# Softmax probabilities copied into a float32r tile by a transfer, and transposed from there

## The chip, the cores and the metric

One core of a Trainium2 chip runs the whole program. Its engines have queues of their own: PE (matrix products and transposes), DVE (VectorE), ACT (ScalarE), POOL (GpSimd), and SP, which in this kernel does nothing but start transfers. The metric is the device time of one execution in microseconds. Instructions of one engine run in the order in which they were built; between engines, semaphores hold them.

## The reference

Two layers of a decoder trunk over 512 tokens of width 1024, batch 1, in float32. In each layer a combined projection feeds three groups of attention heads; their normalised outputs go through one output projection; a SwiGLU feed-forward part and a gated per-layer embedding follow. What the change touches is the softmax of two groups, eight sparse heads (two branches each, over selected blocks and over a window) and four forgetting heads:

```python
def masked_softmax(logits, mask):
    l = jnp.where(mask, logits, NEG_INF)
    m = jnp.max(l, axis=-1, keepdims=True)
    e = jnp.where(mask, jnp.exp(l - m), 0.0)
    return e / jnp.maximum(jnp.sum(e, axis=-1, keepdims=True), TINY)
...
        p_s = masked_softmax(s_s.reshape(b, g_, hpg, tq, n_sel * NSA_SLC_LEN), mask_s)
        o_s = jnp.einsum('bghtnk,bgtnkd->btghd', p_s.astype(vs.dtype), vs)
...
        p_w = masked_softmax(s_w, mask_w)
        o_w = jnp.einsum('bghtk,bkgd->btghd', p_w.astype(vw.dtype), vw)
        o = gt[..., 0:1] * o_c + gt[..., 1:2] * o_s + gt[..., 2:3] * o_w
...
        p = masked_softmax(logits, s_idx[None, :] <= t[:, None])
        return jnp.einsum('bhts,bshd->bthd', p.astype(v.dtype), v)
```

## The kernel before

Float32 products run as passes over operands split into two float32r tiles: a high part (the value rounded to float32r) and the remainder, so that hi x hi, hi x lo and lo x hi add up to nearly float32. Weights come from DRAM as raw tiles (`wraw`, three buffers), ACT writes the high part and DVE or POOL the remainder (`halves`, lines 197 to 201) into `whl` (five buffers).

The attention of a layer is written as generators that are woven with projections, each at its share of the other's progress: the first group of four sparse heads runs beside the query projection of the second and two projections of the forgetting heads, the second group beside further projections and the first part of the output projection, the forgetting heads beside more of the output projection. A scheduler in the tile framework then fixes the order on each engine by priority and by its own estimate of when things are ready; nothing is reordered at run time.

`softmaxes(items)` (line 752) holds the three steps of an item, which is a query tile of 128 rows with one to four softmaxes side by side over at most 512 columns:

- `scores`: PE makes the scores in a PSUM bank and adds the mask (lines 766 and 768). DVE takes the maximum (L771), ACT the exponential with its sum (L774) into a tile `p` (six buffers), DVE the reciprocal of the sum (L776, L777), and POOL scales the row with it and with the branch's gate (L779). The tile `p` is float32.
- `transposes`: PE transposes the blocks of 128 columns of `p` into one PSUM bank `pTp`, one to four of them (L787); ACT writes the high part from there (L792) and DVE the remainder (L793).
- `values`: PE multiplies what is there with v (L983 for the sparse heads, L839 for the forgetting ones).

A loop calls them so that the scores of an item stand three steps ahead of its transposes, and these two steps ahead of its products with v:

```python
            look, lag = 3, 2
...
            for st in range(n + look + lag):
                if st < n:
                    yield scores(items[st])
                if 0 <= st - look < n:
                    yield transposes(items[st - look])
                if 0 <= st - look - lag < n:
                    it = items[st - look - lag]
                    yield it["values"]() if it["values"] else 0
```

A layer has 60 items: 22 for each group of sparse heads, 16 for the forgetting heads. All transfers are started from SP's queue, in its order: the weights, the small vectors, and the swaps `sw` (lines 451 and 452), which copy a head's stack of queries or keys within SBUF with its two halves of 64 partitions exchanged. In the same kernel PE transposes float32r tiles too, the stacks of queries and keys, through the float32r identity `identr` (L442, PSUM tile `stk`).

Of the kernel before, what the change touches and what calls it, by code (L numbers as in the profile page):

```python
# [19 lines left out]
P = 128  # L20
# [13 lines left out]
SCRATCH = 1024     # Pool starts no DMAs  # L34
LN_EXP = "natural_log_exp_and_others"

# Columns of the input projection.
# [5 lines left out]
def hybrid_trunk_kernel(  # L43
# [8 lines left out]
    """float32 products run as three float32r passes over operands split exactly into a high part  # L52
    (the float32r rounding) and the remainder: hi*hi + hi*lo + lo*hi. Where both halves fit on the
    partitions of one operand, the fourth product comes along."""
# [3 lines left out]
    def bc(ap, n):  # L58
        """A row of DRAM on all partitions."""
        return bass.AP(tensor=ap.tensor, offset=ap.offset, ap=[[0, P], [1, n]])  # L60

    def f(ap):
        return ap.bitcast(F32)
# [12 lines left out]
    def utile(shape, dt=F32R, name="u"):  # L76
        """One of the 8 KiB slots that all larger tensors share."""
        return upool.tile(list(shape), dt, name=name, tag="u", bufs=15)

    class Lazy(dict):  # L80
        """Tiles made when first used, so that slots are taken in the order of use."""
# [24 lines left out]
    # how far ahead of the order of the program: evacuations, norms, the per-layer embedding  # L106
    OFE, OFN, OFP = 100, 50, 200

    def weave(*streams):
        """Trace streams (generator, total work) side by side, each at its share of the others' progress."""  # L110
# [17 lines left out]
    @contextlib.contextmanager  # L128
    def prio(off):
        """What is traced here counts as off instructions earlier in the order of the program."""  # L130
        c = tc.cur_priority
        tc.cur_priority = c - off
        yield
        tc.cur_priority += off

# [72 lines left out]
    def weights(w, kts, c0, c, per):  # L208
        """Row tiles kts (that follow each other) of w[:, c0:c0+c] as [P, (hi, lo), tile, column], `per`
        of them in a tile; yields them one by one."""  # L210
# [16 lines left out]
    def project(act, w, kts, c0, c, evac, tags="ddss", tail=2):  # L227
        """Token-major product of act(k, half, token tile) with w[:, c0:c0+c]: the row tiles of w go
        by once, all token tiles taking part; the last ones token tile by token tile. Columns up to
        256: two token tiles share a bank."""  # L230
# [24 lines left out]
        for tt in range(NT):  # L255
# [9 lines left out]
            # a bank that two tiles share is read when both are whole  # L265
# [5 lines left out]
    def project_rows(act, w, kts, c0, c, evac, tag="d", ws=None):  # L271
        """The same, token tile by token tile, the weights staying."""
# [9 lines left out]
    def project_T(act, w, c0, evac, tags):  # L282
        """256 columns of w, weights stationary: [128 columns, t] twice. The last row tiles bank by bank."""
# [22 lines left out]
    sums, early, latest = {}, {}, {}  # L306
    junk = const.tile([P, 768 + 512], BF16, name="junk")      # nothing reads it
# [9 lines left out]
    def begin_rms(tt, n):  # L317
        """The part of the mean square that the first n columns make, ahead of the rest, and where the gain
        is at hand its product with the first half."""
# [18 lines left out]
    def load_gain(gain):  # L338
        """The next norm's gain on all partitions."""
# [5 lines left out]
    def normed(g):  # L345
        """The halves of the rows of RMSNorm of h."""
        first = last_act[0] is None
        for tt in range(NT):
# [4 lines left out]
            # where the next tile's last products are on their way, they go first  # L353
            act_after, dve_after = (tc.issue_after(x) if tt + 1 in done else ExitStack()
                                    for x in done.get(tt + 1, (None, None)))
            # at the start, what comes in late does not hold up what is there already
# [15 lines left out]
    def norm_T():  # L372
        """RMSNorm of h, transposed, in two parts; as act(k, half, token tile or None for all)."""
# [26 lines left out]
    def rope(acc, c, nh, tt, out, dup=1):  # L400
        """Rotary embedding of nh heads at acc[:, c:]; out [P, nh, (dup,) 64]."""
# [15 lines left out]
    def split_heads(src, nh, scale=1.0):  # L417
        """[P, nh, (hi | lo), 64] of scale * src [P, nh, 64]."""
# [5 lines left out]
    def split_v(src, dst):  # L424
        """dst [P, heads, (hi | lo), 64] of src [P, heads, 64]."""
# [12 lines left out]
    def stack(t, nh, dsts):  # L438
        """Transposes [tok, (hi | lo)] of nh <= 4 heads; dsts: (destination, heads) in turn."""
# [8 lines left out]
    def swap(src):  # L448
        """The stack with its halves exchanged."""
# [5 lines left out]
    # =================== mixer ===================  # L455
    def mixer(i):
# [24 lines left out]
        def compress(which, pos, w1, w2):  # L481
# [38 lines left out]
            # tanh form of gelu: x / (1 + exp(-2u)), u = sqrt(2/pi) (x + 0.044715 x^3)  # L520
# [64 lines left out]
        def head_out(head, o):  # L585
            """o: [(o.hi | o.lo), t]; its two halves are added up."""
# [9 lines left out]
        def pair_out(pr, half, o):  # L596
            """The same for half of the queries of both heads, o: [(o.hi | o.lo), query tile, head, query]."""
# [28 lines left out]
        def sb_heads():  # L626
            # kv tiles, each with its first query and first column, that share a bank
            groups = (((3, 256, 0), (2, 256, 256)), ((1, 128, 0),), ((0, 0, 0),))
            items = []
            for hd in range(4):  # L630
                parts = {}      # kv tile -> its softplus, first query, first column
# [90 lines left out]
        def forget_rows():  # L722
            """Rows that bring c_t - c_s into the scores, c the running sum of log-sigmoid."""
# [589 lines left out]
```

## Time and profile before

| | |
|---|---|
| runs | 1585.79, 1592.13 and 1586.5 us; median 1586.5 |
| span of the profiled execution | 1585.9 us (the time around it isn't listed; the median is 0.6 us above the span) |
| PE busy | 1516.4 us, 96% of the span |
| DVE, ACT, POOL busy | 748.0, 735.1 and 576.4 us |
| transfers | 134.58 MB in 114449 packets |
| softmax attention | about 176 to 340 us in layer 0, 961 to 1122 us in layer 1 |

Busy time of PE is modelled: products are pipelined, and a record's length is more than the time until the next one can start. What a product costs PE is therefore read from start to start, or from the chain of waits, which gives each piece the time up to the next.

### The profile page before, as it was taken

Reading aid. Unit: us, or ns where it says so; the run is one execution under the profiler, and the core shown is the slowest. Engines: PE = TensorE matmul, PEld = TensorE weight load, DVE = VectorE, ACT = ScalarE, POOL = GpSimd, SP = SyncE. Lnnn points to the kernel's source line nnn. Section 1 sums busy time; section 2 is a strip of 40 time slices with the busy share of each in tenths; the row PEclk is TensorE's granted clock in tenths of the full one; section 3 lists DMA queues with packets and bytes.
Section 4 is the critical chain, followed back from the end, with each engine's and each line's share of the span. In section 5 each row is a group of like instructions: output and inputs, shape, how many; then the busy total and the mean of one; then the engine's idle time right before and its main releaser. Section 6 shows DMA issues by size and latency. Waiting matters only on the chain.

```text
span 1585.9 us, 23185 instructions
## 1 busy us (share of the span) xinstructions
PE 1516.4 (96%) x8630; PEld 1286.7 (81%) x8630; DVE 748.0 (47%) x1584; ACT 735.1 (46%) x1561; POOL 576.4 (36%) x636
## 2 busy tenths in 40 slices
PE   6899999999999999999988999999999999999997
PEld 6788887878888888888977988778798888888887
DVE  6677869763111111214366778697711121112153
ACT  5476676654333332323353776586533333323243
POOL 4233455453323333321223134555433333323223
PEclk9999999999999999999999999999999999999999
DMA  5421321132333333332224212211233333333221
GB/s 161 116 75 39 81 69 34 48 94 67 93 95 101 98 93 120 119 94 67 81 69 122 56 50 72 79 29 53 81 94 94 93 94 104 101 113 120 93 68 66
DMA packets 114449, 134.58 MB, mean 85 GB/s; under 512 B 6864, under 2 KB 91936, under 8 KB 114336
## 3 DMA queue, kind: packets, MB, share of 16 engines
q1 hardware_dynamic: 114336, 133.10, 28.6%
q8 instruction: 68, 1.11, 0.3%
q14 instruction: 45, 0.37, 0.1%
HBM read 122.59 MB, written 2.10 MB: 79 GB/s over the span
## 4 chain that ended last, share of the span: by engine, by line
PE 77%; DVE 12%; ACT 3%; issue 3%; POOL 3%; DMA 1%; POOLq 0%; ACTq 0%; DVEq 0%
PE gu L224 10%; PE gu L223 10%; PE gu L222 10%; PE acc L223 6%; PE acc L222 6%; PE acc L224 6%; PE accr L222 3%; PE accr L223 2%; PE sc L766 2%; PE accr L224 2%; PE pTp L787 2%; PE no L983 2%; PE ge L222 1%; PE ge L224 1%; PE ge L223 1%
## 5 line engine op out<-in xcount | busy, mean ns | idle before, releaser
L201 POOL TENSOR_TENSOR whl<-wraw,whl 128x512 fp32r<-128x512 f32 (+2 forms) x248 | 333.2, 1348 | 721.0 <-ACT whl L198 617.3
L198 ACT ACTIVATE whl<-wraw 128x512 fp32r<-128x512 f32 (+2 forms) x416 | 260.7, 630 | 490.0 <-PE gu L224 290.3
L201 DVE TENSOR_TENSOR whl<-wraw,whl 128x512 fp32r<-128x512 f32 x168 | 127.1, 758 | 507.0 <-ACT whl L198 506.5
L224 PE MATMUL gu<-xT,whl 128*128 128x512 f32 (+1 forms) x768 | 287.4, 374 | 0.0
L223 PE MATMUL gu<-xT,whl 128*128 128x512 f32 (+1 forms) x768 | 287.2, 374 | 0.0
L222 PE MATMUL gu<-xT,whl 128*128 128x512 f32 (+1 forms) x768 | 286.8, 373 | 0.0
L223 PEld LDWEIGHTS gu<-xT,whl 128*128 128x128 f32 x768 | 144.2, 188 | 27.5
L224 PEld LDWEIGHTS gu<-xT,whl 128*128 128x128 f32 x768 | 144.2, 188 | 27.4
L222 PEld LDWEIGHTS gu<-xT,whl 128*128 128x128 f32 x768 | 144.4, 188 | 27.1
L223 PE MATMUL acc<-whl,hid 128*128 128x512 f32 x352 | 139.6, 397 | 0.0
L222 PE MATMUL acc<-whl,hid 128*128 128x512 f32 x352 | 139.6, 397 | 0.0
L224 PE MATMUL acc<-whl,hid 128*128 128x512 f32 x352 | 138.8, 394 | 0.0
L779 POOL TENSOR_SCALAR p<-p,rc,gt 128x128 f32<-128x128 f32 (+3 forms) x128 | 79.3, 631 | 70.4 <-DVE rc L777 20.8
L774 ACT ACTIVATE p<-sc,mx 128x128 f32<-128x128 f32 (+3 forms) x160 | 83.9, 536 | 22.3 <-DVE mx L771 20.2
L792 ACT ACTIVATE pT<-pTp 128x512 fp32r<-128x512 f32 (+2 forms) x120 | 62.1, 527 | 40.2 <-PE pTp L787 38.8
L793 DVE TENSOR_TENSOR pT<-pTp,pT 128x512 fp32r<-128x512 f32 (+2 forms) x120 | 70.5, 595 | 21.4 <-ACT pT L792 20.4
L224 PEld LDWEIGHTS acc<-whl,hid 128*128 128x128 f32 x352 | 66.3, 188 | 15.4
L223 PE MATMUL acc<-whl,xT 128*128 128x256 f32 x256 | 73.6, 288 | 5.3 <-DVE whl L201 5.3
L222 PEld LDWEIGHTS acc<-whl,hid 128*128 128x128 f32 x352 | 66.2, 188 | 15.1
L223 PEld LDWEIGHTS acc<-whl,hid 128*128 128x128 f32 x352 | 66.1, 188 | 15.3
L222 PE MATMUL acc<-whl,xT 128*128 128x256 f32 x256 | 74.3, 293 | 2.6 <-DVE sv L427 2.0
L224 PE MATMUL acc<-whl,xT 128*128 128x256 f32 x256 | 74.5, 292 | 0.0
(300 smaller groups left out, 3300.7 us busy)
## 6 DMA issues: line engine op xcount, KB each, us to landing
wraw<-in_w_ffn_gate_dram SPq DMA_DIRECT2D x44, 512.0 KB, 3.8
wraw<-in_w_ffn_up_dram SPq DMA_DIRECT2D x44, 512.0 KB, 3.8
wraw<-in_w_ffn_down_dram SPq DMA_DIRECT2D x44, 512.0 KB, 3.7
wraw<-in_w_in_dram SPq DMA_DIRECT2D x36, 512.0 KB, 3.8
wraw<-in_w_out_dram SPq DMA_DIRECT2D x16, 512.0 KB, 3.7
wraw<-in_w_ple_gate_dram SPq DMA_DIRECT2D x16, 512.0 KB, 3.4
sw<-nq SPq DMA_DIRECT2D x32, 128.0 KB, 2.4
wraw<-in_w_in_dram SPq DMA_DIRECT2D x8, 280.0 KB, 2.9
```

What stands on the lines that cost most here:

```text
L198: se.activation(whl[:, 0], raw[:, lo:lo + n], AF.Copy)
L201: eng.tensor_tensor(whl[:, 1], raw[:, lo:lo + n], f(whl[:, 0]), op=ALU.subtract)
L222: i = te.matmul(acc, lhsT=lh, rhs=rh, start=start, stop=False, skip_group_check=True)
L223: te.matmul(acc, lhsT=lh, rhs=rl, start=False, stop=False, skip_group_check=True)
L224: te.matmul(acc, lhsT=ll, rhs=rh, start=False, stop=stop, skip_group_check=True)
L766: te.matmul(s[:, c:c + w], lhsT=lhsT, rhs=rhs, start=(j == 0), stop=False, skip_group_check=True)
L774: se.activation(e[:, u * n:(u + 1) * n], s[:, u * n:(u + 1) * n], AF.Exp, bias=mx[:, u:u + 1], accum_out=sm[:, u:u + 1])
L779: ge.tensor_scalar(e[:, u * n:(u + 1) * n], e[:, u * n:(u + 1) * n], rc[:, u:u + 1], gates[u] if gates else 1.0, op0=ALU.mult, op1=ALU.mult)
L787: te.transpose(pt[:, kt, :], e[:, kt * P:(kt + 1) * P], ident)
L792: se.activation(hi, src, AF.Copy)
L793: ve.tensor_tensor(lo, src, f(hi), op=ALU.subtract)
L983: te.matmul(o[:, qt % 2], lhsT=nv5[:, g, br, kt].rearrange("p t d -> p (t d)"), rhs=pT[:, j, u, kt], start=False, stop=(br == 1 and kt == ...
```

## The change

The probabilities still arrive in the float32 tile `p`. After POOL's scaling a transfer on SP's queue copies them, word for word, into a new tile `er` of type float32r (two buffers), and the transposes read `er`, with the float32r identity and a float32r PSUM tile. The scores now stand four steps ahead of the transposes. The rest of the diff removes comments, which moves line numbers by three after line 780: the transposes are on L790, their evacuations on L795 and L796, the products with v on L842 and L986.

```diff
-            look, lag = 3, 2
+            look, lag = 4, 2
...
                 for u in range(k):
                     ge.tensor_scalar(e[:, u * n:(u + 1) * n], e[:, u * n:(u + 1) * n], rc[:, u:u + 1],
                                      gates[u] if gates else 1.0, op0=ALU.mult, op1=ALU.mult)
+
+                it["e"] = er = upool.tile([P, 512], F32R, name="er", tag="er", bufs=2)
+                nc.sync.dma_start(f(er[:, :k * n]), e[:, :k * n])
                 return sum(w for _, w, _, _ in prods) + k * P / 2
...
             def transposes(it):
                 nb, e = it["k"] * (it["qt"] + 1), it["e"]
-                pt = bank("t", (P, 4, P), name="pTp")
+                pt = bank("t", (P, 4, P), F32R, name="pTp")
                 for kt in range(nb):
-                    te.transpose(pt[:, kt, :], e[:, kt * P:(kt + 1) * P], ident)
+                    te.transpose(pt[:, kt, :], e[:, kt * P:(kt + 1) * P], identr)
                 hi, lo = it["dst"]()
-                src = pt[:, :nb, :]
+                src = f(pt[:, :nb, :])
```

Outside the softmax attention the order on every engine stays as it was. The first place is PE in the second group of sparse heads of layer 0, around the items of three blocks. Before (`accr` is the output projection, `sc` the scores, `no` the products with v):

```order
L787 MATMUL pTp<-ident,p 128x128 x3
L983 MATMUL no<-pT,nv 128x256
L768 LDWEIGHTS identb
L768 MATMUL sc<-cmaskb,identb 128x128
L223 MATMUL accr<-whl,on_1479 128x512
L766 MATMUL sc<-nk,nq_2193 128x256
L766 MATMUL sc<-nk,sw 128x256
L766 MATMUL sc<-nk,nq_2193 128x256
L766 MATMUL sc<-nk,sw 128x256
L787 MATMUL pTp<-ident,p 128x128 x3
L983 MATMUL no<-pT,nv 128x256 x7
L787 MATMUL pTp<-ident,p 128x128 x3
```

The same items after; the three groups of three blocks are again one item each, and follow one another:

```order
L790 MATMUL pTp<-identr,er 128x128 x3
L986 MATMUL no<-pT,nv 128x256
L224 MATMUL accr<-whl,on_1479 128x512
L766 MATMUL sc<-nk,nq_2224 128x512
L766 MATMUL sc<-nk,sw 128x512
L986 MATMUL no<-pT,nv 128x256 x6
L790 MATMUL pTp<-identr,er 128x128 x3
L986 MATMUL no<-pT,nv 128x256
L768 LDWEIGHTS identb
L768 MATMUL sc<-cmaskb,identb 128x2x128
L766 MATMUL sc<-nk,nq_2224 128x512
L790 MATMUL pTp<-identr,er 128x128 x3
```

The transposes of an item now read `er`, and the scores between them belong to items further ahead. The second place is SP's queue in the same stage. Before, it holds weight loads (`wraw`) and swaps (`sw`) alone; the names in brackets are the semaphores that each waits for (`DMAHW` are earlier transfers):

```order
L194 DMA wraw<-in_w_out_dram 128x2x512 [waits DMAHW7_49,Pool_49]
L194 DMA wraw<-in_w_out_dram 128x2x512 [waits DMAHW0_49,Pool_49]
L194 DMA wraw<-in_w_out_dram 128x2x512 [waits DMAHW4_49,DMAHW1_49,Pool_49]
L451 DMA sw<-fqk_2887 64x512 [waits DMAHW2_49,DVE_49,PE_49]
L452 DMA sw<-fqk_2887 64x512 [waits DMAHW3_49,Activation_49]
```

After, each copy waits for POOL (its probabilities) and for PE (the transposes of the item two before it, out of the same buffer of `er`):

```order
L194 DMA wraw<-in_w_out_dram 128x2x512 [waits Pool_49]
L194 DMA wraw<-in_w_out_dram 128x2x512 [waits DMAHW6_49,Pool_49]
L783 DMA er<-p 128x512 [waits DMAHW2_49,DMAHW7_49,PE_49,Pool_49]
L783 DMA er<-p 128x512 [waits DMAHW4_49,PE_49,Pool_49]
L194 DMA wraw<-in_w_out_dram 128x2x512 [waits DMAHW3_49,DMAHW1_49,Pool_49]
L783 DMA er<-p 128x512 [waits DMAHW7_49,PE_49,Pool_49]
L783 DMA er<-p 128x384 [waits DMAHW0_49,PE_49,Pool_49]
L783 DMA er<-p 128x384 [waits DMAHW2_49,PE_49,Pool_49]
```

Between the weight loads now stand 120 copies over both layers, and ten times in each layer a copy stands directly behind a weight load.

## Rows read from the trace of the kernel before

**Rows 1.** The page: busy time of each engine, and the chain by engine.
```profile
PE 1516.4 (96%) x8630; PEld 1286.7 (81%) x8630; DVE 748.0 (47%) x1584; ACT 735.1 (46%) x1561; POOL 576.4 (36%) x636
...
PE 77%; DVE 12%; ACT 3%; issue 3%; POOL 3%; DMA 1%; POOLq 0%; ACTq 0%; DVEq 0%
```

**Rows 2.** Spans and granted clock of the cores.
```profile
core 0: 1585.9 us, clock 0.993
```

**Rows 3.** Windows: the three softmax stages of layer 0, columns in the first line.
```profile
core 0: us, PE busy (x) PEld busy (x) DVE busy (x) ACT busy (x) POOL busy (x), PEclk, DMA share, GB/s
175.00:225.00 50.00, 49.45 (x362) 43.07 (x362) 39.79 (x121) 36.08 (x95) 29.03 (x38) 1.00 0.23 65
254.00:292.00 38.00, 36.93 (x251) 30.39 (x250) 34.64 (x89) 31.23 (x79) 23.87 (x37) 1.00 0.16 43
297.00:337.00 40.00, 37.67 (x218) 30.93 (x217) 27.86 (x72) 23.93 (x60) 21.54 (x25) 0.98 0.32 93
```

**Rows 4.** Timeline of PE: start, length, what; four transposes amid a stage, then at its end.
```profile
270.76 0.60 PE L787 MATMUL pTp<-ident,p 128*128 128x128 f32 x4
...
335.57 1.12 PE L787 MATMUL pTp<-ident,p 128*128 128x128 f32 x4 [2.33 <-POOL p L779]
```

**Rows 5.** Instructions on tile pTp: count, ns min/median/max, first and last start, forms.
```profile
L787 PE MATMUL pTp<-ident,p x400: 270/273/476, 175.8 to 1119.8; 128*128 128x128 f32 x134
L792 ACT ACTIVATE pT<-pTp x120: 257/583/671, 176.5 to 1120.1; 128x512 fp32r<-128x512 f32 x64, 128x384 fp32r<-128x384 f32 x40, 128x128 fp32r<-128x128 f32 x8, 128x256 fp32r<-128x256 f32 x8
```

**Rows 6.** The chain of waits around eight transposes: start, us up to the next.
```profile
223.88 0.23 PE accT L224
224.11 0.87 PE pTp L787 x8
224.98 0.12 PE no L983
```

**Rows 7.** Instructions on tile stk, the float32r transposes.
```profile
L442 PEld LDWEIGHTS stk<-identr,heads x96: 137/139/146, 109.1 to 978.8; 128*128 128x128 f32 x96
L442 PE MATMUL stk<-identr,heads x96: 222/247/285, 109.2 to 978.9; 128*128 128x128 f32 x96
```

**Rows 8.** Timeline of PE around two groups of four float32r transposes.
```profile
155.12 0.53 PE L442 MATMUL stk<-identr,heads 128*128 128x128 f32 x4
155.49 0.35 PE L222 MATMUL acc<-whl,xT 128*128 128x256 f32 x1
155.68 0.28 PE L223 MATMUL acc<-whl,xT 128*128 128x256 f32 x1
...
192.39 0.46 PE L442 MATMUL stk<-identr,heads 128*128 128x128 f32 x4
192.69 0.35 PE L766 MATMUL sc<-nk,nq 128*128 128x256 f32 x1
192.87 0.28 PE L766 MATMUL sc<-nk,sw 128*128 128x256 f32 x1
```

**Rows 9.** Transfers by line: count, KB each, median us from issue to landing.
```profile
sw<-nq SPq DMA_DIRECT2D x32, 128.0 KB, 2.4
...
wraw<-in_w_in_dram SPq DMA_DIRECT2D x8, 260.0 KB, 2.8
...
sw<-sqk SPq DMA_DIRECT2D x16, 128.0 KB, 2.7
sw<-fqk SPq DMA_DIRECT2D x16, 128.0 KB, 2.3
...
out_dram<-xn SPq DMA_DIRECT2D x4, 256.0 KB, 2.0
```

**Rows 10.** Waits of SP's queue: for whom, us in total, times, longest.
```profile
SPq L194 <- POOL whl L201: 818.6, 189, 23.3
```

## The prediction

> **What bounds the kernel now.** I read the page's busy shares and chain first, then the clock, then the busy time of the attention stages, and last the waits and single instructions in them. PE is busy in 96% of the span and carries 77% of the chain that ended last; no other engine passes 47%, and DMA carries 1% of the chain [rows 1]. The granted clock is 0.993 over the run, so PE is at its upper level, 2.4 GHz, nearly throughout [rows 2]. The change touches only the attention heads with a softmax. There PE is busy for 49.45 of 50.00 us, 36.93 of 38.00 and 37.67 of 40.00 in the three stages of layer 0, and DVE is already at 34.64 of 38.00 in the second [rows 3]. So a nanosecond less on PE is worth nearly a nanosecond there, as long as the probabilities arrive in time. Where they don't, PE stands: at the end of the forgetting heads it waits 2.33 us for POOL's last scaling, and the four transposes after it take 1.12 us where four elsewhere take 0.60, since the clock had dropped to its lower level (the stage's mean is 0.98) [rows 3, 4].
>
> **The change, part by part.** The sum is made against the profiled span of 1585.9 us; the median of the runs shown is 1586.5, so 0.6 us lies around it.
>
> *Transposes.* There are 400, in 64 groups of four (the evacuations of 512 columns), 40 of three, 8 of two and 8 of one [rows 5]. On the chain a run of eight float32 transposes takes 0.87 us, 0.109 each [rows 6], so all 400 take 43.6 us. The float32r form stands in the trace too, in the stacks of queries and keys [rows 7]. Where its inputs are at hand, four take 0.30 us to the start of the next product, and that product then takes 0.18 us to its successor instead of the 0.12 of 256 columns [rows 6, 8]: 0.36 us in all against 0.436. Where they aren't, it is 0.37 plus 0.07, or 0.44: no gain [rows 8]. With some 0.085 us from one to the next I take 0.36, 0.275, 0.19 and 0.105 us for four, three, two and one. The saving is 64 x 0.076 + 40 x 0.052 + 8 x 0.028 = 7.2 us. Bounds: 0 (all like the worse group) to 400 x (0.109 - 0.07) = 15.6 us, if all went at the spacing inside the better group, (0.46 - 0.247) / 3 = 0.07 us [rows 7, 8]. I take 7.
>
> *The copies.* 120 transfers on SP's queue, of 64 to 256 KB. The trace has none of this shape within SBUF; the nearest are 128 KB within SBUF (2.4 us to landing), 260 KB from DRAM (2.8) and 256 KB to DRAM (2.0) [rows 9]. I take 2.5 us for most: a little over the SBUF row, since twice the bytes move. The Trainium skill, "DMA: Bandwidth & Descriptors", section "Anatomy of one DMA — SWDGE (gpsimd) path", has a fixed 2.0 us plus bytes over 436 GB/s (for the GpSimd path), which by estimate is 2.6 us for 256 KB; the SBUF row agrees (2.4 us against 2.3 by the page), the row of 256 KB to DRAM doesn't (2.0). By 2.6 us the ring below would cost some 12 us and the whole sum would come to about 1591 us.
>
> *The ring of two.* The copies go into two buffers, so the copy for an item waits until PE has transposed the item two before it (the PE wait on each copy in the order shown with the diff). From the start of that last transpose to the first new one there pass 0.25 us until it is whole, the copy, and 0.14 us of weight load [rows 7]: 2.9 us with 2.5 for the copy, or 2.8 of other PE work in between. In the PE order shown for the second group there stand, between the groups of three at its two ends, two products with values (0.24 us), one of 512 columns of the output projection (0.23), three of scores (0.69), six more with values (0.72), a group of three transposes (0.28) and a mask (about 0.1): 2.26 us by the durations of [rows 6, 8]. So PE waits there about 0.5 us. Counted alike over both layers, 42 of 108 such stretches are under 2.8 us; adding the shortfalls in turn, each delay also giving time to the copy behind it, makes 9 us (1.5, 1.9 and 1.1 in the three stages of a layer). At 2.0 us to landing it is 1 us, at 2.8 us 18.6. I take 9. Behind a waiting transpose all of PE's work is queued; behind a waiting copy, on SP, the swaps of the next heads and the weight loads.
>
> *Looking four ahead instead of three.* In the built order the scores of an item stand further ahead of its transposes, for the last item of the forgetting heads about twice as far. That should remove most of the 2.33 us wait at the end of layer 0 and the slow clock behind it, and some of the same in layer 1: I take 3 us off (bounds 0, if the copy eats it, and 8).
>
> *The rest.* POOL, ACT and DVE do the same work. The copies add about 26 MB to 134 and stand in stages where the DMA engines are 16 to 32% busy [rows 3], so they cost the weights little. SP's order costs something: ten times in each layer a copy stands directly behind a weight load that waits for POOL. I put 2 us on it; DVE near its limit in the second group is within that (bounds 0 and 25, see the third rival).
>
> *Sum:* -7 + 9 - 3 + 2 = +1 us on the span, so 1587 us for the run.
>
> **The rivals.** *The copies are hidden.* If a copy lands in 2.0 to 2.3 us, the ring costs 1 to 2 us and the sum is -7 + 2 - 3 = -8: 1578 us. For it: 256 KB to DRAM took 2.0 us. Against it: no transfer within SBUF has a median under 2.3, with half the bytes [rows 9]. A branch of it has the float32r transposes at 0.07 us each as well: 8 us more, 1570.
>
> *The ring decides (slower).* Place: the second NSA group, where 12 of 20 stretches are short. Price: with 2.8 us to landing the ring costs 18.6 us, and the longer look saves 1 us instead of 3, so -7 + 18.6 - 1 + 2 = +13: 1599 us. It decides from a landing of 2.7 us on, where it alone costs 15. For it speaks the 260 KB row at 2.8; against it that this row reads DRAM, and in pieces half as large as a copy's, and that a PE that waits elsewhere leaves the ring more time.
>
> *SP's order decides (slower).* Weight loads wait 189 times for POOL, 818.6 us in all, 4.3 each and up to 23.3 [rows 10]. If a third of such a wait falls on the copy behind each of the 20 loads and PE has nothing else, 20 x 1.4 = 28 us replace the ring's 9 and the 2: -7 + 28 - 3 = +18, so 1604 us. Against it: the waits of before are those of a queue that ran ahead, and most loads are ready before the copy behind them has its probabilities.
>
> *Transposes aren't what holds PE.* If DVE's 34.64 of 38 us in the second group [rows 3] sets the pace, neither term counts in full and the time stays at 1585 to 1589; this falls within the forecast.
>
> **How the numbers follow.** Gain and ring nearly cancel: 0.52 for a time between 1579 and 1594. Hidden copies have 0.16, their branch with the faster transposes 0.03, the ring 0.18, SP's order 0.11. A measurement of this kernel can tell about 0.5%, 8 us, from no change; so the first two give 0.19 faster (1578 lies just past that edge), the ring and SP's order 0.29 slower, and 0.52 is left for no change. The forecast's own terms give 1579 to 1594; with the other cases the range is 1574 to 1604, which leaves out the fast branch below and about half of SP's order, with the ring's far end, above.
>
> **What would show it.** Right: the float32r group on line 790 at 0.08 to 0.09 us per transpose on the chain; copies landing in 2.4 to 2.6 us; PE waiting for the copies some 30 to 50 times, each under 1 us, most in the second group; no 2.33 us wait at the end of the forgetting heads. Wrong: copies at 2.0 us and no such waits (faster); copies at 2.8, or SP waiting for POOL with a copy behind it and PE idle for 2 us and more with the clock down (slower); or a transpose spacing of 0.109 as before, which would leave only the costs.

## The result, and the profile after

The changed kernel takes 1607.8 us (median of 4, 1603.7 to 1610.3) against 1588.6 before in the same comparison: ratio 1.0114, 95% interval 1.0097 to 1.0132, so 18 us slower (15 to 21). The forecast was 1587, the range ended at 1604. The profiled execution has a span of 1605.6 us, 19.7 more than before.

The page of the changed kernel, against [rows 1], and its span and clock, against [rows 2]:

```profile
PE 1526.8 (95%) x8630; PEld 1292.4 (80%) x8630; DVE 751.4 (47%) x1584; ACT 737.9 (46%) x1561; POOL 575.1 (36%) x636
...
PE 73%; DVE 12%; ACT 5%; issue 3%; POOL 3%; DMA 3%; POOLq 0%; ACTq 0%; DVEq 0%; SPq 0%
```

```profile
core 0: 1605.6 us, clock 0.985
```

PE has lost four points of the chain, DMA and ACT have gained two each, and the clock is 0.985 instead of 0.993. Windows of the changed kernel that hold the three softmax stages of layer 0 (columns as in [rows 3]):

```profile
177.00:235.00 58.00, 52.57 (x363) 45.17 (x362) 42.36 (x115) 36.18 (x93) 28.67 (x37) 0.94 0.45 146
264.00:302.00 38.00, 35.74 (x234) 29.59 (x234) 32.87 (x87) 29.19 (x74) 21.48 (x30) 0.96 0.43 146
306.00:350.00 44.00, 41.99 (x243) 33.36 (x242) 28.95 (x75) 26.99 (x64) 24.24 (x32) 1.00 0.41 132
```

In the first, PE stands 5.4 of 58 us, where it stood 0.55 of 50, and the clock is 0.94 instead of 1.00. By the timeline, the stretch from the first group's compressed scores to the second's grew from 69.6 to 77.3 us in layer 0 and from 69.6 to 75.5 in layer 1: 13.8 of the 19.7 us. I had put the largest part of the ring's cost, 1.9 of 4.5 us a layer, into the second group.

What PE waited for there: its timeline in the changed kernel (start, length, what, and in brackets the wait and who ended it), which answers to [rows 4]:

```profile
178.85 0.54 PE L790 MATMUL pTp<-identr,er 128*128 128x128 f32 x4 [1.03 <-DMA er<-p]
...
183.43 0.89 PE L790 MATMUL pTp<-identr,er 128*128 128x128 f32 x7 [1.17 <-DMA er<-p]
...
219.13 0.45 PE L790 MATMUL pTp<-identr,er 128*128 128x128 f32 x3 [1.90 <-DVE pT L796]
...
234.74 0.50 PE L790 MATMUL pTp<-identr,er 128*128 128x128 f32 x4 [1.03 <-DMA er<-p]
...
349.20 0.53 PE L790 MATMUL pTp<-identr,er 128*128 128x128 f32 x4 [0.78 <-DMA er<-p]
```

The first two are the first and the third item of the group: their copies left within 0.03 us of POOL's end, so no ring held them, and too little other work covered their landing, which took 2.28 us for the first and 3.38 us for the third, with a weight load started 1.07 us ahead of it. The fourth had a late copy, as the chain of the changed kernel shows (start, us, what):

```profile
230.07 4.53 DMA er<-p
...
234.74 0.50 PE pTp L790 x4
```

The third wait is not for a copy; it comes back below, with e8. The last is the end of the forgetting heads: the 2.33 us of [rows 4] are gone, 0.78 for a copy stand there instead. PE's waits in all (for whom, us, times, longest; before, no line names a copy, and the transposes waited 3.7 us, 4 times, for POOL):

```profile
PE pTp L790 <- DMA er<-p: 8.7, 10, 1.2
...
PE sc L766 <- ACT p L774: 4.6, 4, 2.1
PE pTp L790 <- DVE pT L796: 4.6, 4, 1.9
```

To see the whole loss I added up the start-to-start times of PE's instructions in the attention stages of both layers: what exceeds a product's usual time by over 0.25 us ("standing"), what the lower clock added, and the transposes themselves, in us.

| kernel | standing | of it ahead of transposes | ahead of scores | lower clock | transposes |
|---|---|---|---|---|---|
| before | 16.4 | 7.7 | 6.6 | 1.5 | 35.5 |
| after | 31.7 | 18.8 | 6.1 | 8.1 | 30.6 |
| e7 (no copies, three ahead) | 17.7 | 7.5 | 6.6 | 3.6 | 32.5 |
| e8 (no copies, four ahead) | 25.7 | 7.4 | 9.2 | 6.7 | 31.4 |
| e16 (ring of three) | 29.9 | 16.8 | 8.8 | 4.9 | 31.2 |

After against before: 15.3 more standing, 6.6 more for the clock, 4.9 less for the transposes, 17 of the 19.7 us. The profiled executions are not the median ones: e8's and e16's were the slowest of theirs, e7's the fastest.

The copies by size, against [rows 9], and the waits of SP's queue, against [rows 10]:

```profile
er<-p SPq DMA_DIRECT2D x64, 256.0 KB, 2.3
er<-p SPq DMA_DIRECT2D x40, 192.0 KB, 2.1
```

```profile
SPq L194 <- POOL whl L201: 745.1, 192, 26.2
...
SPq L783 <- PE pTp L790: 105.3, 84, 4.8
SPq L783 <- POOL p L779: 37.2, 29, 7.9
...
SPq L783 <- DMA er<-p: 14.0, 10, 2.2
```

These are waits, and a copy can have more than one: 84 were ended by the ring (PE's transposes out of the buffer), 29 by POOL, 10 by the landing of an earlier copy. Matched copy by copy in the trace, 112 of the 120 left within 0.3 us of the later of their own two conditions, 91 times the ring's and 21 times POOL's. Two stood behind a weight load for about 1 us.

### The profile page after: what moved, and what is told of

The parts are those of the page before. It is cut to its first block, busy times and chain, and to the rows that moved or that the text cites. A ratio compares the mean times of both kernels' runs of the same rounds, so it can differ in the third digit from the quotient of the medians.

```text
span 1605.6 us, 23403 instructions
## 1 busy us (share of the span) xinstructions
PE 1526.8 (95%) x8630; PEld 1292.4 (80%) x8630; DVE 751.4 (47%) x1584; ACT 737.9 (46%) x1561; POOL 575.1 (36%) x636
## 3 DMA queue, kind: packets, MB, share of 16 engines
q1 hardware_dynamic: 131616, 159.32, 31.7%
## 4 chain that ended last, share of the span: by engine, by line
PE 73%; DVE 12%; ACT 5%; issue 3%; POOL 3%; DMA 3%; POOLq 0%; ACTq 0%; DVEq 0%; SPq 0%
PE gu L224 10%; PE gu L223 10%; PE gu L222 10%; PE acc L222 6%; PE acc L223 6%; PE acc L224 6%; PE accr L222 2%; PE accr L223 2%; PE accr L224 2%; DMA er<-p 2%; PE sc L766 2%; PE no L986 2%; PE ge L222 1%; PE ge L223 1%; PE ge L224 1%
## 5 line engine op out<-in xcount | busy, mean ns | idle before, releaser
L223 PEld LDWEIGHTS gu<-xT,whl 128*128 128x128 f32 x768 | 144.2, 188 | 27.5
L774 ACT ACTIVATE p<-sc,mx 128x128 f32<-128x128 f32 (+3 forms) x160 | 83.4, 528 | 25.4 <-DVE mx L771 19.7
L796 DVE TENSOR_TENSOR pT<-pTp,pT 128x512 fp32r<-128x512 f32 (+2 forms) x120 | 71.3, 597 | 34.9 <-ACT pT L795 33.0
L795 ACT ACTIVATE pT<-pTp 128x512 fp32r<-128x512 f32 (+2 forms) x120 | 62.4, 525 | 51.2 <-PE pTp L790 50.1
```

The costliest lines, as they stand in the source:

```text
L223: te.matmul(acc, lhsT=lh, rhs=rl, start=False, stop=False, skip_group_check=True)
L774: se.activation(e[:, u * n:(u + 1) * n], s[:, u * n:(u + 1) * n], AF.Exp, bias=mx[:, u:u + 1], accum_out=sm[:, u:u + 1])
L795: se.activation(hi, src, AF.Copy)
L796: ve.tensor_tensor(lo, src, f(hi), op=ALU.subtract)
```

## The experiments

Eighteen kernels ran. The theories: A, a copy's own time between POOL and PE; B, the ring of two; C, the order that four ahead gives; D, the transposes gain nothing; E, traffic and queue order; F, late landings beside weight loads; G, more in flight. Below, a ratio is to the kernel before on the same chip, whose median moved between 1588.6 and 1590.0; 0.0010 is 1.6 us.

| run | look | transposes | copies, ring | median us | ratio, 95% interval |
|---|---|---|---|---|---|
| e15 | 2 | f32r | none | 1592.2 | 1.0019, 1.0010 to 1.0028 |
| **e7** | 3 | f32r | none | 1581.5 | 0.9956, 0.9939 to 0.9972 |
| e2 | 3 | f32r | 2 | 1610.6 | 1.0129, 1.0114 to 1.0145 |
| e3 | 4 | f32 | none | 1595.0 | 1.0029, 1.0017 to 1.0041 |
| e5 | 4 | f32 | 2, not read | 1596.2 | 1.0047, 1.0033 to 1.0061 |
| e8 | 4 | f32r | none | 1595.9 | 1.0045, 1.0029 to 1.0061 |
| after | 4 | f32r | 2 | 1607.8 | 1.0114, 1.0097 to 1.0132 |
| e16 | 4 | f32r | 3 | 1599.7 | 1.0061, 1.0041 to 1.0081 |
| e17 | 4 | f32r | 4 | 1599.2 | 1.0056, 1.0035 to 1.0077 |
| e12 | 5 | f32r | none | 1596.6 | 1.0050, 1.0035 to 1.0065 |
| e11 | 5 | f32r | 2 | 1615.0 | 1.0176, 1.0154 to 1.0199 |
| e18 | 5 | f32r | 4 | 1599.1 | 1.0062, 1.0042 to 1.0081 |

**The look-ahead alone (e3).**

```diff
-            look, lag = 3, 2
+            look, lag = 4, 2
```

> The kernel before with a look-ahead of four, no copies, float32 transposes. Theory A: the 2.33 us wait at the end of the forgetting heads and the stretch at the lower clock behind it (1.7 us) go, some back for waits on DVE: 1584 to 1589 us. Theory C: the two waits for DVE of 2.1 us are here too, with one stretch at the lower clock each: 1593 to 1597 us.

1595.0 us: by the ratio 4.6 slower (2.7 to 6.5), where I had forecast 3 faster. The wait at the end of the forgetting heads went, as forecast, but another came. From its timeline, and its list of PE's waits (us, times, longest; before: 4.6, 2, 2.3 on the first line, and no second):

```profile
336.08 0.38 PE L839 MATMUL fo<-pT,fv 128*128 128x256 f32 x1 [1.50 <-ACT pT L792]
```

```profile
PE sc L766 <- ACT p L774: 6.7, 8, 2.3
...
PE fo L839 <- ACT pT L792: 2.8, 2, 1.5
```

A fourth item ahead means one more set of scores at the start of a group, and the score banks are three: two of the new waits, 0.56 us each, stand at the start of the first group. The time is theory C's, its waits are not: in place of its two waits of 2.1 us for DVE there is one of 0.5 us. Nor do PE's waits make up the loss. In the softmax stages of both layers they add up to 12.7 us against 11.1 before, since most of the 3.7 us for POOL went, and the lower clock, once more in layer 1, costs about 1.7. These stages are 7.0 us longer in the profiled execution; the other 4 us stay open.

**The transposes alone (e7, e8).** The probabilities' own tile becomes float32r:

```diff
-                it["e"] = e = ptile("p")
+                it["e"] = e = upool.tile([P, 512], F32R, name="p", tag="p", bufs=6)
...
-                    ge.tensor_scalar(e[:, u * n:(u + 1) * n], e[:, u * n:(u + 1) * n], rc[:, u:u + 1],
+                    ge.tensor_scalar(e[:, u * n:(u + 1) * n], f(e[:, u * n:(u + 1) * n]), rc[:, u:u + 1],
...
-                pt = bank("t", (P, 4, P), name="pTp")
+                pt = bank("t", (P, 4, P), F32R, name="pTp")
...
-                    te.transpose(pt[:, kt, :], e[:, kt * P:(kt + 1) * P], ident)
+                    te.transpose(pt[:, kt, :], e[:, kt * P:(kt + 1) * P], identr)
```

> The kernel before, look-ahead of three, no copies; the probabilities' own tile is float32r, so ACT's exponentials and POOL's scaled probabilities are rounded as they are written, and the transposes are float32r. Nothing else changes. Transposes as predicted (7.2 us) or as the changed kernel's trace has them (a group of four 0.366 us against 0.439, a group of three 0.336 against 0.339, some 5 us): 1582 to 1585 us. Theory D, they are hidden behind other engines: 1588 to 1590 us.

> The same with a look-ahead of four: the changed kernel without its copies and without their buffers. If look-ahead and transposes add up: 1595.0 - 4 = 1590 to 1591 us, as far as the run with POOL's own float32r tile (1591.4) was not held back by its four buffers; with that hold gone, down to 1586 us.

With three ahead it is 1581.5 us, 7.0 us faster than the kernel before (4.4 to 9.7) and the fastest of all versions; its probabilities are rounded, so it is not the same computation. In its profiled execution the softmax stages of both layers, from the first group's compressed scores to the forgetting heads' last product, are 5.0 us shorter (345.3 against 350.3); by the table 3.0 of them are the transposes' own time. Where the others are saved isn't shown. From its chain, eight transposes, against 0.87 in [rows 6]:

```profile
223.52 0.23 PE accT L224
223.75 0.63 PE pTp L787 x8
224.38 1.02 PE no L983 x8
```

With four ahead it is 1595.9: no gain over float32 with four ahead (e3). The transposes are as fast, but by the table PE stands 8.0 us more than in e7 and the lower clock takes 3.1 us more, 11 of the 14 us between the two. Its waits in e8, and the head norm of DVE (ns min/median/max):

```profile
PE sc L766 <- ACT p L774: 7.4, 6, 2.4
...
PE pTp L787 <- DVE pT L793: 4.0, 2, 2.0
...
PE no L983 <- DVE pT L793: 3.5, 2, 1.8
...
PE fo L839 <- ACT pT L792: 2.7, 2, 1.6
...
PE pTp L787 <- POOL p L779: 0.5, 3, 0.2
```

```profile
L617 DVE SCALAR_TENSOR_TENSOR pair<-pair,hgT,rs x16: 737/754/3246, 137.1 to 1138.3; 128x512 f32<-128x512 f32 x16
```

POOL's lateness (3.7 us in the kernel before) is nearly gone, which is what the longer look-ahead is for; but once in each layer PE waits 2 us for an evacuation that is queued on DVE behind a norm of 3.2 us (1.4 us at most in the kernel before) and 1.8 us for one behind another DVE instruction of 2.9 us (L857, 0.5 us in the middle of the kernel before), and the forgetting heads end late. The changed kernel has the same two waits, one in each layer. DVE there, then POOL, from the timelines of the changed kernel:

```profile
215.24 3.23 DVE L617 SCALAR_TENSOR_TENSOR pair<-pair,hgT,rs 128x512 f32<-128x512 f32 x1
218.40 0.68 DVE L796 TENSOR_TENSOR pT<-pTp,pT 128x512 fp32r<-128x512 f32 x1
...
214.76 0.65 POOL L779 TENSOR_SCALAR p<-p,rc,gt 128x384 f32<-128x384 f32 x1
215.39 2.53 POOL L201 TENSOR_TENSOR whl<-wraw,whl 128x512 fp32r<-128x512 f32 x2
```

The norm began while POOL scaled, and ended only when POOL's two weight remainders were through. With a ring of three (e16) the same norm begins as long before the end of the same scaling (0.17 us), and gets through, while POOL's two take 3.04 us:

```profile
215.49 0.75 DVE L617 SCALAR_TENSOR_TENSOR pair<-pair,hgT,rs 128x512 f32<-128x512 f32 x1
...
215.00 0.66 POOL L779 TENSOR_SCALAR p<-p,rc,gt 128x384 f32<-128x384 f32 x1
215.64 3.04 POOL L201 TENSOR_TENSOR whl<-wraw,whl 128x512 fp32r<-128x512 f32 x2
```

The Trainium skill, "SBUF — State Buffer", section "Summary: rules for kernel authors", says that of a DVE instruction with two SBUF inputs and a GpSimd one that reads SBUF, the second to start is blocked until the first is through. The traces fit it in part: in each pair one side is longer, 3.23 us against 0.75 or 3.04 against 2.53. By that rule alone the norm would have gone on once the scaling was through, after 0.17 us. In one run it stood aside for two further POOL instructions and in the other it didn't; the traces don't show why, nor the blocking itself.

**POOL's own float32r tile (e4).** POOL writes its result into `er` (four buffers, four of `p`), and no copy is made.

```diff
+                it["e"] = er = upool.tile([P, 512], F32R, name="er", tag="er", bufs=4)
...
-                    ge.tensor_scalar(e[:, u * n:(u + 1) * n], e[:, u * n:(u + 1) * n], rc[:, u:u + 1],
+                    ge.tensor_scalar(er[:, u * n:(u + 1) * n], e[:, u * n:(u + 1) * n], rc[:, u:u + 1],
...
-                it["e"] = er = upool.tile([P, 512], F32R, name="er", tag="er", bufs=2)
-                nc.sync.dma_start(f(er[:, :k * n]), e[:, :k * n])
```

> POOL writes the scaled probabilities straight into the float32r tile (four buffers, four of the unscaled ones), which rounds them, so their remainders are lost; no copies; look-ahead of four, float32r transposes. Theory A: the copy's whole cost goes and the transposes' gain stays: 1588.6 - 5 for the transposes - 2 for the longer look = 1580 to 1585 us. Theory C: about 1591 us. Theory D, float32r transposes gain nothing in place: the same as the look-ahead of four alone, within 2 us.

1591.4 us, ratio 1.0014 (1.0000 to 1.0027). No norm over 1.5 us stands in its trace; but PE waited 12.5 us for score banks (4.6 before), with four buffers of `p` and of `er`. It tells nothing sure of the theories.

**The copies' traffic (e5).**

```diff
-                it["e"] = er = upool.tile([P, 512], F32R, name="er", tag="er", bufs=2)
+                er = upool.tile([P, 512], F32R, name="er", tag="er", bufs=2)
...
-                pt = bank("t", (P, 4, P), F32R, name="pTp")
+                pt = bank("t", (P, 4, P), name="pTp")
...
-                    te.transpose(pt[:, kt, :], e[:, kt * P:(kt + 1) * P], identr)
+                    te.transpose(pt[:, kt, :], e[:, kt * P:(kt + 1) * P], ident)
```

> The changed kernel with its copies, ring of two and look-ahead of four, but the transposes are float32 again and read the probabilities themselves; nothing reads the copies. Theory A, a copy's own time between POOL and PE is the cost: PE no longer waits for it, so as the look-ahead of four alone, 1595 us, within 3. Theory E, the copies cost by their traffic or by their place on SP's queue: near the changed kernel plus the transposes' 4 us, 1605 to 1612 us.

1596.2 us, 1.2 over e3 (2.9 by the ratios, 0 to 6): copies that nobody waits for are nearly free. That refutes a cost by traffic, and by copies that hold up the weights and swaps behind them while they wait for POOL. It doesn't test a copy that leaves late because a weight load stands ahead of it, since nothing here waits for a copy; against that speaks the count of the 120 copies above. Nor does it test copies that wait on SP for PE's transposes, since PE reads none.

**The look-ahead with copies (e2, e11, e12).** The line `look, lag` alone, at 3 and at 5 in the changed kernel and at 5 in e7's.

> The change with the old look-ahead of three. Theory A: one item less of PE work lies between an item's scores and its transposes, some 1.7 to 2.5 us, about the time of a copy, so nearly every copy comes late: 1615 to 1630 us. Theory C, the new order (four ahead) is what costs: the two waits of 2.06 and 2.08 us for DVE go, and the stretch at the lower clock behind one of them: about 1602 us.

> The changed kernel with a look-ahead of five. The copies cost 1610.6 - 1581.5 = 29 us at three and 12 at four. Theory A, it is the time from POOL's end to PE that they take out of what the look-ahead gives: at five some 5 us more than the next run. A cost of another kind (the order, the ring): still about 12.

> Float32r probabilities without copies, look-ahead of five. The look-ahead itself has cost 6 us from three to four with float32 and 14 with float32r; with three score banks a fifth item ahead has nowhere to go but a wait: 1596 to 1605 us.

With three ahead the copies cost 29 us over e7 (27.5 by the ratios), and the whole is 2.4 us slower than with four (by the ratios, within the two intervals). PE's waits for them in e2:

```profile
PE pTp L790 <- DMA er<-p: 18.6, 23, 1.9
```

That fits theory A, if 4 us below its range, and refutes C as the whole cause: by it the copies with three ahead would be cheaper than with four. That four ahead has a cost of its own without copies stands, by e3 and e8. Five ahead then refuted the plain form of A: 18 us over e12 instead of 5, and in e11:

```profile
PE pTp L790 <- DMA er<-p: 18.3, 12, 3.0
```

**The ring (e1, e6, e13, e16, e17, e18).** The line below, at 3 (e6, e16) or 4; with it `bufs` of `p` at 4 (e1) or 5 (e13, e17, e18).

```diff
-                it["e"] = er = upool.tile([P, 512], F32R, name="er", tag="er", bufs=2)
+                it["e"] = er = upool.tile([P, 512], F32R, name="er", tag="er", bufs=3)
```

> Four buffers for the copies instead of two (and four for the probabilities instead of six, to make room). Theory A, each copy's own time on the path: in the changed kernel's trace PE stands 17.5 us in all ahead of transposes; 6.8 of that is for copies that left as soon as POOL was done, 6.0 for copies that had waited for a buffer, 4.1 for two items held by DVE. Four buffers take away the 6.0 and one or two of the five stretches at the lower clock in the attention stages (1.7 us each): 1607.8 - 6.0 - 2.5 = about 1599 us. Theory B, the ring of two is the cause: what is left is the transposes' gain, 1588.6 - 5 + 3 = about 1587 us.

> The changed kernel with a ring of three and all six buffers of probabilities kept (the room comes from a scratch tile that nothing reads). In the run with four and four, waits for a free probabilities buffer may have hidden a gain: PE waited 8.6 us for score banks there, 4.6 in the changed kernel. Theory B, the ring of two costs the 6.0 us of waits that followed a buffer: 1600 to 1602 us. Theory A, a copy that leaves earlier is followed by an item whose probabilities are late, or lands later: 1605 to 1608 us.

> The changed kernel with four buffers for the copies and a look-ahead of five at once (five buffers of probabilities). Theory A, a copy's own time, held back by the ring when the look-ahead is long and by POOL's end when the ring is long: with both limits lifted the copies cost some 5 us over the same look-ahead without copies (1596.6), so 1598 to 1603 us. Theory G, more in flight makes copies land later and cost more: 1608 us or more.

These gave 1607.0, 1607.1 and 1610.7 us, and seemed to clear the ring. They were confounded. In e1 only four buffers of `p` were left, and PE waited 8.6 us for score banks; e17 below, with five, is 7.8 us faster. In e6 and e13 I had made room by cutting a scratch tile of the norms so that two norms' parts met; PE's waits for the norms, 11.3 us in the changed kernel, are in e6:

```profile
PE xnT L380 <- DVE xn L368: 18.1, 6, 8.5
```

In e13 they are 19.0 us. Against the runs below that tile cost 7.4 us (e6) and 11.6 (e13). With its parts laid so that they don't meet (e6 and e13 had `0:hi - lo` there):

```diff
-    junk = const.tile([P, 768 + 512], BF16, name="junk")
+    junk = const.tile([P, 1024], BF16, name="junk")
...
-        latest["square"] = se.activation(junk[:, j:j + hi - lo], ...
+        latest["square"] = se.activation(junk[:, lo:hi], ...
```

> The changed kernel with three buffers for the copies, all six of probabilities, and the scratch tile's two parts laid so that they don't meet. If the ring of two is a cost of its own: 1607.8 - 5 = about 1602 us (the attention stages of the spoilt run were 5.2 us shorter). If it isn't, since a copy that leaves earlier only lands later: 1606 to 1608 us.

> The same with four buffers for the copies and five of probabilities. Nearly every copy then leaves at POOL's end, and what is left over 1595.9 (the same without copies) is a copy's own time. Theory A with a part for the ring: 1600 to 1602 us. No cost of the ring: 1606 to 1608 us.

> The same with a look-ahead of five. If the longer look-ahead covers a copy's own time once the ring allows it: within 5 us of the same without copies (1596.6), 1598 to 1602 us. If the copies cost what they cost at four: 1604 us or more.

1599.7, 1599.2 and 1599.1 us. So the ring of two costs 8.4 us (some 4 to 13) at four ahead and 16 to 18 at five (no run has the new scratch tile with a ring of two, but PE's waits for the norms are 11.8 us in e16 and 11.3 in the changed kernel); and with the ring open, the copies cost little over the same look-ahead without them: 2.5 us at four (e16 against e8), 1.9 at five (e18 against e12), by the ratios and both within their uncertainty. The traces ask for care about where the 8 us lie. SP's waits, and PE's, in e16:

```profile
SPq L783 <- POOL p L779: 83.2, 64, 7.9
SPq L783 <- PE pTp L790: 74.1, 55, 4.3
```

```profile
PE pTp L790 <- DMA er<-p: 9.2, 10, 2.2
...
PE sc L766 <- ACT p L774: 7.2, 5, 2.4
...
PE pTp L790 <- DVE pT L796: 1.7, 2, 0.9
```

PE's waits in e17, then in e18:

```profile
PE pTp L790 <- DMA er<-p: 11.7, 12, 2.1
PE sc L766 <- ACT p L774: 8.4, 5, 2.4
```

```profile
PE sc L766 <- ACT p L774: 10.3, 8, 2.3
...
PE pTp L790 <- DMA er<-p: 4.3, 4, 1.5
```

With three buffers more copies leave at POOL's end (64 of SP's waits against 29; copy by copy 67 against 21), yet PE waits for them as long as before, 9.2 and 11.7 us against 8.7. What e16 saves over the changed kernel in its attention stages is, by the table, 3.2 us of the lower clock and 1.8 of standing: the wait behind the norm is gone (4.6 to 1.7 us) and that for score banks has grown. So the ring's cost is shown by the runs, but not as the waits that I had counted. The two profiled executions are only 4.5 us apart, which the table accounts for; the rest of the 8.4 us, which is between the medians, no trace can place. That an open ring as such keeps the norm from its collision isn't shown either: e1, with four buffers, has it in one layer. And since e8 carries that collision too, the copies' 2.5 us over e8 are too small a price for them; their own waits are 9 to 12. Only five ahead with an open ring brings these down, to 4.3, and pays for it at the score banks.

**Weight loads beside copies (e9, e10).**

```diff
+        if thin[0]:
+            if not fixed:
+                fixed.append(wpool.tile([P, 1024], F32, name="wfix", tag="wfix", bufs=1))
+                nc.sync.dma_start(fixed[0], w_in[0, 0:P, 0:1024])
+            return fixed[0]
-        raw = wpool.tile([P, 1024], F32, name="wraw", tag="wraw", bufs=3)
+        raw = wpool.tile([P, 1024], F32, name="wraw", tag="wraw", bufs=2)
```

> The changed kernel, but the mixers' products take all their weights from one tile that is loaded once, so that no weight load is on the DMA queue beside the copies (the mixers' products are then of other weights; the raw-weight buffers elsewhere are two instead of three). To be read against the next run, which is the same without copies: with weight loads the copies cost 1607.8 - 1595.9 = 12 us. Theory F, what costs is that a copy beside a weight load lands late (in the changed kernel 31 such copies took 2.9 us in the middle and up to 4.5, the nine alone 1.8 to 2.3): the difference of the two falls to 2 to 6 us. Theory A, the 2.3 us that a copy takes in any case: it stays at 9 us or more.

> The float32r probabilities without copies, look-ahead of four, with the mixers' weights from one tile loaded once as in the run before. Theory F: 2 to 6 us faster than that run; theory A: 9 us or more.

1600.9 (1.0087, 1.0064 to 1.0111) and 1593.8 us (1.0028, 1.0014 to 1.0041): the copies cost 9 us by the ratios (5 to 14) without the loads, 11 with them. The two theories aren't told apart. That copies land late beside a weight load is seen in the trace of the changed kernel; what it costs isn't told.

**Each item copied twice (e14).**

```diff
-                nc.sync.dma_start(f(er[:, :k * n]), e[:, :k * n])
+                mid = upool.tile([P, 512], F32, name="mid", tag="mid", bufs=2)
+                nc.sync.dma_start(mid[:, :k * n], e[:, :k * n])
+                nc.sync.dma_start(f(er[:, :k * n]), mid[:, :k * n])
```

> The changed kernel with every item copied twice in a row, into a middle tile (ring of two) and from there into the float32r tile (five buffers of probabilities). Theory A: another 2.3 us for every item; the copies' 11 us become 25 to 40: 1620 to 1635 us. If the cost lay in the traffic or the queue's order, which the copies that nothing reads didn't show, or in float32r tiles: 1608 to 1613 us.

1709.1 us, far past both: a second copy costs 101 us (some 10 of them by the scratch tile, which was that of e6). SP's waits in it fit a reason, since both hops stand in one queue and the second waits for the first:

```profile
SPq L785 <- DMA mid<-p: 70.3, 64, 3.2
SPq L784 <- DMA er<-mid: 63.5, 61, 3.6
```

Behind each such wait all later copies stand. That these 134 us on SP are the 101 isn't shown: PE's own waits for the copies are 29.1 us there, and the mean granted clock is 0.965. What the times of the runs do show is that the copies' cost isn't a price per copy: one copy per item costs between 2.5 us (e16) and 29 (e2), by how far the items' distance and the ring cover its time, and a second one 101 more.

**Two ahead (e15).** e7 with `look, lag = 2, 2`.

> Float32r probabilities without copies, look-ahead of two instead of three. If what the look-ahead costs is the order that it gives to DVE's and ACT's work, and shorter is always better: 1575 to 1580 us. If three is where POOL's end just comes in time (a slack of 3 us in the middle over the items of the kernel before, with some 2 us per item): PE waits for POOL, 1590 us or more.

1592.2 us: PE waits for POOL more often than with three ahead (4.2 us, 6 times):

```profile
PE pTp L787 <- POOL p L779: 6.7, 17, 1.2
```

These 2.5 us more are a quarter of the 10 that separate it from e7 by the ratios; the rest isn't placed. Without copies three ahead is the best of two to five; with them, and the ring of two, four is about as good (1607.8) as three (1610.6), and five is worse (1615.0).

## Why the prediction was wrong

*What bounds the kernel:* right. Where PE stands in these stages, the time grows.

*Transposes, -7:* the size was right at three ahead: -7.0 us (e7; 4.4 to 9.7), 0.079 us each on the chain where I had 0.08 to 0.09. At four ahead they gain nothing: float32r against float32 (e8 against e3) is +0.0016 in the ratio, within the two intervals, and PE waits the more. I had no term for this.

*Looking four ahead, -3:* **this is the step that failed**, in sign. I priced what the longer distance removes, POOL's lateness and the 2.33 us, and both went. What it brings I had bounded at nothing lost ("bounds 0 and 8"): waits for score banks, 1.5 us for an evacuation at the end of the forgetting heads, and, with float32r, DVE's norm against POOL's weight remainders. It costs 4.6 us with float32 and 14 with float32r (e8 against e7). So the -10 for these two steps became +7 (e8's ratio of 1.0045), 17 us off, which is the whole miss (+1 forecast, +18 measured). The copies' 11 us on top of e8 are what ring and rest had been given. This is the split in the order of the sum, whose ring was worked out for four ahead. The steps don't add up the same in another order: put on e7 at three ahead the copies cost 27.5 us, and the longer look then gives 2.4 back (e2, changed kernel), not clear of noise. What the sum missed either way is that the longer look, put in to cover the copies, costs about as much as it saves them. The waits named above make some 8 of e8's 14 us and the lower clock 3; the rest stays open.

*The ring of two, +9:* 8.4 us by e16, so the size was right, but by luck, as the working wasn't. The landing was 2.3 us, not 2.5, with a tail to 4.5, and PE waited 10 times, not 30 to 50, most of it in the first group. I had left out the group's first items, whose copies no ring holds, and the spread of the landings: with a weight load in flight 31 copies took 2.9 us in the middle, 14 of them over 3. And what an open ring saves isn't PE's waits for copies.

*The rest, +2:* e5 has 1 to 3 us more than e3, right as far as its interval (0 to 6) tells.

*The rivals:* "copies are hidden" fell; a landing of 2.3 us was thought enough for it. "The ring decides" has the right direction and about half of the loss (8.4 of 18 us), though at a landing of 2.3 us, not from 2.7 on. "SP's order decides" came nearest in time (1604) for a wrong reason: 112 of 120 copies left within 0.3 us of what POOL and the ring allowed. "Transposes aren't what holds PE" fell at three ahead (e7) and fits at four, where they gain nothing.

*Open:* whether the ring of two causes the norm's collision or the order merely falls so; and what brings the clock down. In the attention it is at its lower level (1.2 GHz) four times in layer 0 and once in layer 1, before once and never; each time within 2.3 us after a wait of PE of 0.9 to 2.1 us. But waits of 1.9 and 2.1 us in layer 1 of the changed kernel (at 1013 and 1048 us) and one of 2.3 us at 245 us of the kernel before didn't bring it down. By the table the clock has 6.6 us of the loss, a term that my sum didn't have.

## What to carry to other kernels

A change of three edits has three prices: build each alone, and each pair, and time them before the sum is believed, above all the edit that was put in to help another. Here the prices didn't add up: with float32r transposes the longer look cost 14 us without the copies and nothing that shows with them. A longer look-ahead isn't a free cover; every ring that the items pass (score banks, probabilities, copies) has to have room for it, and each in-order engine gets another order. When room is made for an experiment, what it is taken from needs a control, or the verdict is on the room.

## What the runs showed that was not expected

- A DVE instruction of 0.75 us with two SBUF inputs took 3.23 us beside POOL's scaling and two weight remainders, and 0.75 us (e16) with the same three at the same distance within 0.02 us. What decides isn't seen in the traces; it is worth 2 us of PE each time, and more with the clock.
- A copy of 256 KB within SBUF lands after 2.3 us, 64 KB after 1.8; with a 512 KB weight load in flight up to 4.5.
- Twice the transfers on the way of each item made the program 101 us slower, once 12 to 29.
